# One Hymba-style encoder layer: the last MLP group by seven products, in the PSUM banks of the group in front of it

## The chip, the cores and the metric

The kernel runs on one NeuronCore of a Trainium2 chip. The metric is the device time of one execution in microseconds (us). The kernel before takes 780.66 us, the median of 3 runs (780.21 to 782.45).

## The reference, cut to what matters

The layer normalises x (512 tokens of 1024), projects it, runs two groups of attention heads, a cross-attention and an MLP, and normalises the result. The change touches only the second half of the MLP and the last norm:

```python
    u = rmsnorm(h, norm_ff_g[l]) @ w1[l]          # 512 x 4096
    h = h + jnp.square(jax.nn.relu(u)) @ w2[l]    # w2 is 4096 x 1024
return rmsnorm(h, final_norm_g)
```

## The kernel before

**Groups.** The hidden width of 4096 is cut into eight groups of 512 (`g` = 0 to 7, `NG` = 8). For a group, `mlp_up` makes four PSUM tiles of 128 hidden rows by 512 tokens, and `square` turns each into squared ReLU in SBUF (`sq`, two tiles of [128, 2, 512] per group). The way down multiplies these 512 hidden units by a 512 x 1024 piece of `w2` and adds the result to the residual, which is kept in four SBUF tiles `acc0` to `acc3` of 128 tokens by 1024.

**Numbers as high and low parts.** Every operand of a matmul is split in two: ACT writes a rounded copy (`hi`, line 166 for weights, `hidden_part` for the hidden side), DVE the remainder (`lo`, line 168). A product takes three matmuls: hi times hi, hi times lo, lo times hi (lines 1289 to 1291). The stationary operand is the hidden side (`hb`), the moving one the weight (`whd`, `wld`).

**Seven products instead of eight.** For groups 0 to 6 the way down is a 2 x 2 block product made with seven half-sized products (`PRODUCTS`, in the order "1", "2", "6", "5", "7", "3", "4") instead of eight. Its four weight blocks are loaded as `a1`, `c1`, `a2`, `b2`, `b1` into eight buffers that go round (`slots`, inside the tiles `wq0` and `wq1`), by DMAs of the SP queue. Sums of weight blocks are made by DMAs that add into SBUF (`add_weights`, on the POOL queue). Sums of hidden blocks are made on DVE (`hidden_sums`). One product is 12 matmuls of 128 x 512: two token halves `t`, two slices `k`, three matmuls. Its result goes through one of the banks U, Y and V (two of each), from which `add_to` adds it to `acc` on DVE.

**The last group.** Group 7 is done plainly: `hidden_plain` splits its four hidden slices, four weight blocks are split without sums, and `plain_down` (lines 1298 to 1307) makes, for each of four token blocks and each of two column halves, 12 matmuls. `last_block` follows a token block at a time: DVE adds the PSUM bank to `acc` (line 1319), ACT squares it and sums along the row (line 1320), POOL adds the two halves' sums and raises to the power -0.5 (lines 1325, 1331), ACT scales one half of the columns (line 1332), DVE the other (line 1334), and ACT and SP each send one half out. The last token block's second column half is done in two pieces of 256 columns.

**What sets the order.** PE's order is the order of the code. On the other engines the order is set when the program is built, from the place in the code, with the splits of weights moved ahead (`ahead(PW)`). At run time every engine takes its instructions strictly in that order, each waiting for its semaphores. `unit` keeps up to four split weight units ready: `whd` and `wld` have four buffers each, so the split of a unit waits until PE is done with the unit four before. The tiles of 4 KB per partition that hold `hb` and `acc` (`s4`) have twelve buffers, `k4` has four.

Of the kernel before, what the change touches and what calls it, by code (L numbers as in the profile page):

```python
# [16 lines left out]
P = 128  # L17
S = 512
# [24 lines left out]
def emit(  # L43
# [1102 lines left out]
    def up_units(g):  # L1146
        for j in range(2):
            spec = panel(w1, g * HG + j * WT)
            for n in range(2):

                def prep(g=g, j=j, n=n, spec=spec):
                    if (j, n) == (0, 0):
                        raws[g - 1] = down_raws(g - 1)
# [15 lines left out]
    def down_raws(g):  # L1169

        w = {}
        for n, name in enumerate(("a1", "c1", "a2", "b2", "b1") if g < NG - 1 else ("a1", "a2", "b2", "b1")):
            r, c = quad[name]
            w[name] = slots[(5 * g + n) % 8]
# [3 lines left out]
        if g < NG - 1:  # L1178
            add_weights(w["a2"], w["b2", "src"])
            add_weights(w["c1"], w["a2", "src"])  # L1180
        return w
# [4 lines left out]
    def down_units(g):  # L1186
        w = {}
        names = PRODUCTS if g < NG - 1 else ("a1", "a2", "b2", "b1")

        def prep(name, n):  # L1190
            if n == 0:
                w.update(raws.pop(g) if g in raws else down_raws(g))
            raw = w[RAW.get(name, name)]
# [8 lines left out]
        for n, name in enumerate(names):  # L1202
            unit_q.append((("d", g, name), lambda name=name, n=n: prep(name, n)))
# [47 lines left out]
    def hidden_plain(g, k):  # L1251
        src = sqs[g, k // 2][:, k % 2, :]
        hb = s4([2, S], f"hb{g}_{k}", R)
        ac.activation(hb[:, 0, :], src, AF.Copy)
        ve.tensor_tensor(hb[:, 1, :], src, f(hb[:, 0, :]), ALU.subtract)
        hbs[g, k] = hb

    def add_to(ps, rows, half, t, sign):
        a = acc[2 * rows + t][:, half * S : (half + 1) * S]
        if sign > 0:  # L1260
            ve.tensor_tensor(a, ps, a, ALU.add)
        else:
            ve.scalar_tensor_tensor(a, ps, -1.0, a, op0=ALU.mult, op1=ALU.add)
# [12 lines left out]
    def mlp_down(g):  # L1276
        banks = {}
        for name in PRODUCTS:
            whi, wlo = unit("d", g, name)
            bank, first_, goes = PLAN[name]  # L1280
            hb = hbs[g, name]
            for t in range(2):
                if first_:
                    banks[bank, t] = {"U": sc, "Y": tr, "V": mm}[bank](f"{bank}{g}{t}")
                ps = banks[bank, t]
                ts_ = slice(t * P, (t + 1) * P)
                for k in range(2):
                    hi, lo = hb[:, 0, k, ts_], hb[:, 1, k, ts_]
                    te.matmul(ps, hi, whi[:, k, :], start=first_ and k == 0, stop=False, skip_group_check=True)  # L1289
                    te.matmul(ps, hi, wlo[:, k, :], start=False, stop=False, skip_group_check=True)  # L1290
                    te.matmul(ps, lo, whi[:, k, :], start=False, stop=k == 1, skip_group_check=True)  # L1291
                for rows, half, sign in goes:
                    add_to(ps, rows, half, t, sign)
            if g + 1 < NG - 1:
                hidden_part(g + 1, name)
            elif PRODUCTS.index(name) < 4:
                hidden_plain(g + 1, PRODUCTS.index(name))

    def plain_down(ps, tb, wts, ns):
        ts_ = slice(tb * P, (tb + 1) * P)  # L1300
        for k in range(4):
            hb = hbs[NG - 1, k]
            whi, wlo = wts[k // 2]
            hi, lo = hb[:, 0, ts_], hb[:, 1, ts_]
            te.matmul(ps, hi, whi[:, k % 2, ns], start=k == 0, stop=False)
            te.matmul(ps, hi, wlo[:, k % 2, ns], start=False, stop=False)
            te.matmul(ps, lo, whi[:, k % 2, ns], start=False, stop=k == 3)

    def last_block(wts, tb, pieces):

        o = k4([D], f"fo{tb}")
        a = acc[tb]
        ms = sm(len(pieces), f"fm{tb}")
        part = None
        for n, (half, ns) in enumerate(pieces):
            ps = mm(f"y{half}{tb}_{ns.start}")[:, ns]
            plain_down(ps, tb, wts[half], ns)
            cs = slice(half * S + ns.start, half * S + ns.stop)
            ve.tensor_tensor(a[:, cs], ps, a[:, cs], ALU.add)
            ac.activation(o[:, cs], a[:, cs], AF.Square, scale=1.0 / 32.0, accum_out=ms[:, n : n + 1])  # L1320
            if part is None:
                part = ms[:, n : n + 1]
            else:
                e = sm(1, f"fe{tb}{n}")
                gp.tensor_scalar(e, ms[:, n : n + 1], part, EPS if n == len(pieces) - 1 else 0.0, op0=ALU.add, op1=ALU.add)
                part = e
        h0, h1 = slice(0, S), slice(S, D)
        ag = t2(f"fa{tb}")
        gp.tensor_tensor(ag, a[:, h0], gfin[0], op=ALU.mult)
        r = sm(1, f"fr{tb}")  # L1330
        gp.tensor_tensor(r, part, mhalf[:, 0:1], op=ALU.pow)
        ac.activation(o[:, h0], ag, AF.Identity, scale=r)
        ac.dma_start(out[tb * P : (tb + 1) * P, h0], o[:, h0])
        ve.scalar_tensor_tensor(o[:, h1], a[:, h1], r, gfin[1], op0=ALU.mult, op1=ALU.mult)
        nc.sync.dma_start(out[tb * P : (tb + 1) * P, h1], o[:, h1])

    def mlp_up_group(g):
        for j in range(2):
            if g < 2:
                wt = next_panel()  # L1340
                if (g, j) == (0, 0):
                    raws[0] = down_raws(0)
# [3 lines left out]
            else:  # L1346
                wt = tuple(list(x) for x in zip(*(unit("u", g, j, n) for n in range(2))))
            yield from mlp_up(g, j, wt)

    for g in range(NG):  # L1350
        if g >= 2:
            up_units(g)
        if g >= 1:
            down_units(g - 1)
    down_units(NG - 1)
# [26 lines left out]
    wts = [[got["a1"], got["b1"]], [got["a2"], got["b2"]]]  # L1382
    halves = [(0, slice(0, S)), (1, slice(0, S))]
    quarters = [(0, slice(0, S)), (1, slice(0, WT)), (1, slice(WT, S))]
    for tb in range(NT):
        last_block(wts, tb, halves if tb < NT - 1 else quarters)
# [28 lines left out]
```

## Time and profile before

| | |
|---|---|
| median of 3 runs | 780.66 us |
| the profiled execution | 779.9 us |
| its span, first to last instruction | 778.2 us |
| granted TensorE clock, mean | 0.998 |
| products of group 6 start | 728.53 us |
| plain matmuls of group 7 start | 747.57 us |
| last matmul starts | 770.51 us |

The profile has one execution. Engines are PE (matmul), PEld (load of the stationary operand), DVE, ACT, POOL, SP. In a timeline a row gives start, duration, engine, line of the kernel, operation, output and inputs, count, and in brackets the idle time of that engine before it with what ended it. A matmul's row of 128 x 512 lasts 0.39 us because matmuls overlap; the distance between two starts is what one costs.

### The profile page before, as it was taken

Reading aid. Unit: us, or ns where it says so; the run is one execution under the profiler, and the core shown is the slowest. Engines: PE = TensorE matmul, PEld = TensorE weight load, DVE = VectorE, ACT = ScalarE, POOL = GpSimd, SP = SyncE. Lnnn points to the kernel's source line nnn. Section 1 sums busy time; section 2 is a strip of 40 time slices with the busy share of each in tenths; the row PEclk is TensorE's granted clock in tenths of the full one; section 3 lists DMA queues with packets and bytes.
Section 4 is the critical chain, followed back from the end, with each engine's and each line's share of the span. In section 5 each row is a group of like instructions: output and inputs, shape, how many; then the busy total and the mean of one; then the engine's idle time right before and its main releaser. Section 6 shows DMA issues by size and latency. Waiting matters only on the chain.

```text
span 778.2 us, 11540 instructions
## 1 busy us (share of the span) xinstructions
PE 767.7 (99%) x4380; PEld 655.1 (84%) x4380; DVE 517.7 (67%) x839; ACT 366.3 (47%) x626; POOL 187.4 (24%) x259
## 2 busy tenths in 40 slices
PE   8999999999999999999999999999999999999996
PEld 6889998988989988888888888888888888888875
DVE  4747755587587656655548656949595868778662
ACT  5655555676474533244434244444353535344433
POOL 7107432424344024410016510101001010100013
PEclk9999999999999999999999999999999999999999
DMA  8553322232544343222113596575758485754302
GB/s 237 196 123 112 97 56 82 81 110 83 163 134 128 121 161 95 94 83 81 55 55 100 205 253 147 147 177 155 177 158 188 140 201 144 194 132 119 71 4 106
DMA packets 80777, 100.43 MB, mean 129 GB/s; under 512 B 4513, under 2 KB 62410, under 8 KB 80722
## 3 DMA queue, kind: packets, MB, share of 16 engines
q1 hardware_dynamic: 72002, 76.08, 32.0%
q0 software_dynamic: 8128, 22.57, 13.6%
q10 hardware_dynamic: 592, 1.05, 0.4%
q8 instruction: 34, 0.56, 0.3%
q14 instruction: 21, 0.17, 0.1%
HBM read 88.14 MB, written 4.21 MB: 119 GB/s over the span
## 4 chain that ended last, share of the span: by engine, by line
PE 94%; DVE 2%; ACT 1%; DMA 1%; POOL 1%; issue 1%; SPq 0%; POOLq 0%; ACTq 0%
PE u L227 7%; PE u L228 7%; PE u L229 7%; PE U L1290 3%; PE U L1289 3%; PE U L1291 3%; PE xq L227 2%; PE xw L227 2%; PE xw L229 2%; PE xq L228 2%; PE xq L229 2%; PE xw L228 2%; PE wo L229 2%; PE wo L227 2%; PE wo L228 2%; PE Y L1290 2%
## 5 line engine op out<-in xcount | busy, mean ns | idle before, releaser
L168 DVE TENSOR_TENSOR wld<-wq,whd 128x1024 fp32r<-128x1024 f32 x49 | 59.7, 1219 | 24.0 <-ACT whd L166 23.9
L228 PE MATMUL u<-x_lo,whu 128*128 128x512 f32 x192 | 74.7, 389 | 0.0
L229 PE MATMUL u<-x_hi,wlu 128*128 128x512 f32 x192 | 74.7, 389 | 0.0
L227 PE MATMUL u<-x_hi,whu 128*128 128x512 f32 x192 | 74.7, 389 | 0.0
L166 ACT ACTIVATE whd<-wq 128x1024 fp32r<-128x1024 f32 x49 | 51.0, 1051 | 23.6 <-PE u L228 23.6
L166 ACT ACTIVATE whu<-wru 128x1024 fp32r<-128x1024 f32 x24 | 25.3, 1053 | 56.9 <-DMA wru<-in_w_dram 56.9
L168 DVE TENSOR_TENSOR wlu<-wru,whu 128x1024 fp32r<-128x1024 f32 x24 | 29.3, 1220 | 26.7 <-ACT whu L166 26.7
L1167 POOL DMA_DIRECT2D wq<-in_w_dram x14 | 17.0, 1217 | 116.6 <-DMA wq<-in_w_dram 113.8
L1167 POOL DMA_DIRECT2D wq<-wq x14 | 12.3, 877 | 134.4 <-DVE wld L168 95.9
L1289 PE MATMUL U<-whd,hb 128*128 128x512 f32 x112 | 43.6, 389 | 0.0
L1290 PE MATMUL U<-wld,hb 128*128 128x512 f32 x112 | 43.6, 389 | 0.0
L1291 PE MATMUL U<-whd,hb 128*128 128x512 f32 x112 | 43.6, 389 | 0.0
L227 PEld LDWEIGHTS u<-x_hi,whu 128*128 128x128 f32 x192 | 36.0, 188 | 7.5
L229 PEld LDWEIGHTS u<-x_hi,wlu 128*128 128x128 f32 x192 | 36.0, 188 | 7.5
L228 PEld LDWEIGHTS u<-x_lo,whu 128*128 128x128 f32 x192 | 36.0, 188 | 7.4
L1227 ACT ACTIVATE sq<-ur 128x512 f32<-128x512 f32 x32 | 19.9, 624 | 29.1 <-DVE ur L1224 29.1
L1224 DVE SCALAR_TENSOR_TENSOR ur<-u,rbc 128x512 f32<-128x512 f32 x32 | 21.9, 688 | 17.5 <-PE u L229 17.5
L862 POOL TENSOR_SCALAR bi<-nF,Ft 128x128 f32<-128x128 f32 (+3 forms) x32 | 21.7, 678 | 43.9 <-PE pv L905 16.8
L879 ACT ACTIVATE bi<-bi,mx 128x128 f32<-128x128 f32 (+3 forms) x32 | 17.9, 560 | 21.9 <-DVE mx L877 21.8
L1289 PEld LDWEIGHTS U<-whd,hb 128*128 128x128 f32 x112 | 21.0, 188 | 4.4
L1291 PEld LDWEIGHTS U<-whd,hb 128*128 128x128 f32 x112 | 21.0, 188 | 4.4
L1290 PEld LDWEIGHTS U<-wld,hb 128*128 128x128 f32 x112 | 21.0, 188 | 4.3
(950 smaller groups left out, 2452.6 us busy)
## 6 DMA issues: line engine op xcount, KB each, us to landing
wq<-in_w_dram SPq DMA_DIRECT2D x39, 512.0 KB, 3.7
wru<-in_w_dram SPq DMA_DIRECT2D x24, 512.0 KB, 3.8
wq<-in_w_dram POOLq DMA_DIRECT2D x14, 512.0 KB, 8.4
wq<-wq POOLq DMA_DIRECT2D x14, 512.0 KB, 4.6
xTd<-xT POOLq DMA_DIRECT2D x4, 512.0 KB, 3.0
nF<-Fd POOLq DMA_DIRECT2D x8, 256.0 KB, 4.3
hT<-xTd POOLq DMA_DIRECT2D x4, 512.0 KB, 4.7
xt<-in_x_dram SPq DMA_DIRECT2D x3, 512.0 KB
```

The costliest lines, as they stand in the source:

```text
L166: ac.activation(hi, raw, AF.Copy)
L168: ve.tensor_tensor(lo, raw, f(hi), ALU.subtract)
L227: te.matmul(ps, wh, hi, start=n_ == 0, stop=False)
L228: te.matmul(ps, wh, lo, start=False, stop=False)
L229: te.matmul(ps, wl, hi, start=False, stop=n_ == KC - 1)
L862: gp.tensor_scalar(bi[:, 0:n], fF[h][:, 0:n], -1.0, Ft[:, tb, h : h + 1], op0=ALU.mult, op1=ALU.add)
L1167: gp.dma_start(raw.rearrange("p (k n) -> p k n", k=2), src, accum_op=ALU.add)
L1224: ve.scalar_tensor_tensor(u, ps, 0.0, rbc2, op0=ALU.max, op1=ALU.mult)
L1227: ac.activation(sqs[g, j][:, i, :], u, AF.Square)
L1289: te.matmul(ps, hi, whi[:, k, :], start=first_ and k == 0, stop=False, skip_group_check=True)
L1290: te.matmul(ps, hi, wlo[:, k, :], start=False, stop=False, skip_group_check=True)
L1291: te.matmul(ps, lo, whi[:, k, :], start=False, stop=k == 1, skip_group_check=True)
```

## The change

Group 7 is made by the same seven products as the others, and it is woven into group 6: after each product of group 6 comes the same product of group 7, into the same PSUM banks, and `add_to` runs only after group 7's. The five weight blocks of group 7 are loaded by `down_raws(NG - 1)`; two of them go into free `k4` tiles. `last_block` is replaced by `finish`, which is called when an (token block, column half) piece of `acc` has had its last addition: after product "2" (blocks 0 and 1, columns 0 to 511), "7" (blocks 2 and 3, columns 512 to 1023), "3" (blocks 0 and 1) and "4" (blocks 2 and 3). A first call makes the sum of squares and the product with the norm's gain for that half; a second call adds the other half's squares, makes the row's factor and sends both halves out. For blocks 2 and 3 the second sum of squares is made on DVE (`tensor_tensor_reduce`) instead of ACT. The very last matmuls (product "4" of group 7, second token half) are done in two pieces of 256 columns. In all groups the addition of `a2` to `a1` is issued with product "1" instead of "2".

```diff
-    def down_raws(g):
-        w = {}
-        for n, name in enumerate(("a1", "c1", "a2", "b2", "b1") if g < NG - 1 else ("a1", "a2", "b2", "b1")):
...
+    def load_raws(g, names):
+        w = raws.setdefault(g, {})
+        for name in names:
             r, c = quad[name]
-            w[name] = slots[(5 * g + n) % 8]
+            n = 5 * g + RAWS.index(name)
+            w[name] = slots[n % 8] if n < 38 else k4([D], f"wq{n}")
...
-            if name == "2":
-                for to, of in (("a1", "a2"), ("b1", "a1")):
-                    add_weights(w[to], w[of].rearrange("p (k n) -> p k n", k=2))
+            if name in ("1", "2"):
+                to, of = (("a1", "a2"), ("b1", "a1"))[int(name) - 1]
+                add_weights(w[to], w[of].rearrange("p (k n) -> p k n", k=2))
...
-    def mlp_down(g):
+    def mlp_down(gs):
+        end = gs[-1] == NG - 1
         banks = {}
-        for name in PRODUCTS:
-            whi, wlo = unit("d", g, name)
+        for n, name in enumerate(PRODUCTS):
             bank, first_, goes = PLAN[name]
...
+            for g in gs:
+                whi, wlo = unit("d", g, name)
+                hb = hbs[g, name]
+                for t in range(2):
+                    if first_ and g == gs[0]:
+                        banks[bank, t] = {"U": sc, "Y": tr, "V": mm}[bank](f"{bank}{g}{t}")
+                    ps = banks[bank, t]
+                    ts_ = slice(t * P, (t + 1) * P)
+                    last = (g, name, t) == (NG - 1, PRODUCTS[-1], 1)
+                    for ns in (slice(0, WT), slice(WT, S)) if last else (slice(0, S),):
+                        for k in range(2):
+                            hi, lo = hb[:, 0, k, ts_], hb[:, 1, k, ts_]
+                            begin = first_ and g == gs[0] and k == 0
...
+                        for rows, half, sign in goes if g == gs[-1] else ():
+                            add_to(ps, rows, half, t, sign, ns)
+                            if end and (name, rows) in FINAL:
+                                finish(2 * rows + t, half, ns)
+            if not end:
+                hidden_part(gs[0] + 1, name)
+            elif n + 1 < len(PRODUCTS):
+                hidden_part(NG - 1, PRODUCTS[n + 1])
+    FINAL = (("2", 0), ("7", 1), ("3", 0), ("4", 1))
+    fin = {}
+    def finish(tb, half, ns):
+        a = acc[tb]
+        cs = slice(half * S + ns.start, half * S + ns.stop)
+        if tb not in fin:
+            e = sm(1, f"fe{tb}")
+            ac.activation(t2(f"fj{tb}"), a[:, cs], AF.Square, scale=1.0 / 32.0, accum_out=e)
+            gp.tensor_scalar(e, e, 1.0, EPS, op0=ALU.mult, op1=ALU.add)
+            ag = t2(f"fa{tb}")
+            gp.tensor_tensor(ag, a[:, cs], gfin[half], op=ALU.mult)
+            fin[tb] = [e, cs, ag, None]
+            return
...
+        if tb < 2:
+            ac.activation(o[:, cs], a[:, cs], AF.Square, scale=1.0 / 32.0, accum_out=v)
+            v0, v = v, sm(1, f"fw{tb}")
+            gp.tensor_scalar(v, v0, e, 0.0, op0=ALU.add, op1=ALU.add)
+        else:
+            ve.tensor_tensor_reduce(out=o[:, cs], in0=a[:, cs], in1=a[:, cs], scale=1.0 / D, scalar=e, op0=ALU.mult, op1=ALU.add, accum_out=v)
+        fin[tb][0] = v
+        if ns.stop < S:
+            ag2 = t2(f"fb{tb}")
+            gp.tensor_tensor(ag2[:, ns], a[:, cs], gfin[half][:, ns], op=ALU.mult)
...
+        r = sm(1, f"fr{tb}")
+        gp.tensor_tensor(r, v, mhalf[:, 0:1], op=ALU.pow)
+        def scale():
...
+            ac.activation(o[:, cs0], ag, AF.Identity, scale=r)
+            ac.dma_start(out[rows, cs0], o[:, cs0])
...
+            if ns.start:
+                p0 = slice(half * S, half * S + ns.start)
+                ve.tensor_scalar(o[:, p0], fin["piece"][:, 0 : ns.start], r, None, op0=ALU.mult)
+            ve.scalar_tensor_tensor(o[:, cs], a[:, cs], r, gfin[half][:, ns], op0=ALU.mult, op1=ALU.mult)
+            nc.sync.dma_start(out[rows, hs_], o[:, hs_])
...
+                if (g, j) == (NG - 1, 0):
+                    down_raws(NG - 1)
...
+        hidden_sums(g)
         if g < NG - 1:
-            hidden_sums(g)
-        mlp_down(g - 1)
-    got = {n: unit("d", NG - 1, n) for n in ("a1", "a2", "b2", "b1")}
...
-    for tb in range(NT):
-        last_block(wts, tb, halves if tb < NT - 1 else quarters)
+            mlp_down((g - 1,))
+    hidden_part(NG - 1, PRODUCTS[0])
+    mlp_down((NG - 2, NG - 1))
```

**ACT, end of its queue.** The rows name the tile written, then the tiles read; the number after `hb` or `whd` is group and product, `fo`, `fa`, `fr` and `fv` carry the token block. Before, the hidden parts are all split ahead of the first row of the final norm:

```order
L1254 ACTIVATE hb7_3_7059<-sq71_6942 128x512
L166 ACTIVATE whd64_7039<-wq0_4782 128x1024
L166 ACTIVATE whd7a1_7066<-wq0_4782 128x1024
L166 ACTIVATE whd7a2_7084<-wq1_4783 128x1024
L166 ACTIVATE whd7b2_7102<-wq1_4783 128x1024
L166 ACTIVATE whd7b1_7120<-wq1_4783 128x1024
L1320 ACTIVATE fo0_7124,fm0_7125<-acc0_4498 128x512 x2
```

After, at the same end of ACT's queue:

```order
L166 ACTIVATE whd74_7209<-wq39_6854 128x1024
L1315 ACTIVATE fj2_7188,fe2_7187<-acc2_4500 128x512
L1315 ACTIVATE fj3_7201,fe3_7200<-acc3_4501 128x512
L1326 ACTIVATE fo0_7232,fv0_0_7233<-acc0_4498 128x512
L1342 ACTIVATE fo0_7232<-fa0_7066,fr0_7237 128x512
L1326 ACTIVATE fo1_7250,fv1_0_7251<-acc1_4499 128x512
L1343 DMA out_0_dram<-fo0_7232 128x512
L1342 ACTIVATE fo1_7250<-fa1_7079,fr1_7255 128x512
L1249 ACTIVATE hb74_7261<-sq71_6952 128x512
L1343 DMA out_0_dram<-fo1_7250 128x512
```

The high part of group 7's product "4" (`hb74`) now stands behind the second sums of squares and the scalings of token blocks 0 and 1.

**DVE, end of its queue.** Before, three rows for each column half and token block; the last two blocks end so:

```order
L1334 SCALAR_TENSOR_TENSOR fo2_7208<-acc2_4500,fr2_7244,gfin1_4779 128x512
L1319 TENSOR_TENSOR acc3_4501<-y03_0_7252,acc3_4501 128x512
L1319 TENSOR_TENSOR acc3_4501<-y13_0_7267,acc3_4501 128x256
L1319 TENSOR_TENSOR acc3_4501<-y13_256_7284,acc3_4501 128x256
L1334 SCALAR_TENSOR_TENSOR fo3_7250<-acc3_4501,fr3_7303,gfin1_4779 128x512
```

After, the last rows are these (ISA is `tensor_tensor_reduce`, and the 128x1 row behind it reads its sum):

```order
L1259 TENSOR_TENSOR acc2_4500<-U60_6998,acc2_4500 128x512
L1259 TENSOR_TENSOR acc3_4501<-U61_7005,acc3_4501 128x256
L1330 ISA fo2_7283,fv2_0_7284<-acc2_4500,fe2_7187 128x512
L1330 ISA fv2_0_7284 128x1
L1330 ISA fo3_7295,fv3_0_7296<-acc3_4501,fe3_7200 128x256
L1330 ISA fv3_0_7296 128x1
L1259 TENSOR_TENSOR acc3_4501<-U61_7005,acc3_4501 128x256
L1348 SCALAR_TENSOR_TENSOR fo2_7283<-acc2_4500,fr2_7286,gfin0_4778 128x512
L1330 ISA fo3_7295,fv3_256_7307<-acc3_4501,fv3_0_7296 128x256
L1330 ISA fv3_256_7307 128x1
L1347 TENSOR_SCALAR fo3_7295<-fb3_7298,fr3_7309 128x256
L1348 SCALAR_TENSOR_TENSOR fo3_7295<-acc3_4501,fr3_7309,gfin0_4778 128x256
```

The sums of squares of blocks 2 and 3 are now on DVE, and the scaling of block 2 stands between the two pieces of block 3. Right ahead of the first of these rows stands the low part of `hb74` (line 1253), and ahead of that the scalings of blocks 0 and 1 (line 1348).

**POOL, from the weight sums of groups 5 to 7 to the first row of the norm.** `in_w2_dram` is an addition from HBM, the others add one SBUF tile to another. Before:

```order
L1167 DMA wq1_4783<-in_w2_dram 128x2x512
L1167 DMA wq0_4782<-in_w2_dram 128x2x512
L1167 DMA wq0_4782<-wq0_4782 128x1024
L1167 DMA wq1_4783<-wq0_4782 128x1024 x2
L1167 DMA wq0_4782<-wq1_4783 128x1024
L1329 TENSOR_TENSOR fa0_7158<-acc0_4498,gfin0_4778 128x512
```

After:

```order
L1167 DMA wq0_4782<-wq0_4782 128x1024
L1167 DMA wq1_4783<-wq0_4782 128x1024
L1167 DMA wq1_4783<-in_w2_dram 128x2x512 x2
L1167 DMA wq1_4783<-wq0_4782 128x1024
L1167 DMA wq0_4782<-wq1_4783 128x1024 x2
L1167 DMA wq39_6854<-wq0_4782 128x1024
L1318 TENSOR_TENSOR fa0_7066<-acc0_4498,gfin0_4778 128x512
```

Two additions from HBM for group 7 now stand ahead of group 6's addition of `a2` to `a1`, and two of group 7's own stand among and behind group 6's.

More of the change, by code (lines that the diff above doesn't have):

```diff
@@ L1249, in hidden_part, with add_to @@
         hbs[g, name] = hb
[L1251 to L1259, printed above, removed]
+    def add_to(ps, rows, half, t, sign, ns):
+        a = acc[2 * rows + t][:, half * S + ns.start : half * S + ns.stop]
         if sign > 0:
[L1261 removed]
+            ve.tensor_tensor(a, ps[:, ns], a, ALU.add)
         else:
[L1263 removed]
+            ve.scalar_tensor_tensor(a, ps[:, ns], -1.0, a, op0=ALU.mult, op1=ALU.add)
     PLAN = {
@@ L1299, in plain_down @@
[L1299 to L1311, printed above, removed]
-        a = acc[tb]
[L1313 to L1329, printed above, removed]
-        r = sm(1, f"fr{tb}")
[L1331 to L1335, printed above, removed]
```

75 lines of the change are left out of this document (37 added, 38 removed).

## The prediction, made before the changed kernel ran

> **What bounds the kernel now.** I read the page first, for the engine that sets the end:
>
> ```profile
> span 778.2 us, 11540 instructions
> ...
> PE 767.7 (99%) x4380; PEld 655.1 (84%) x4380; DVE 517.7 (67%) x839; ACT 366.3 (47%) x626; POOL 187.4 (24%) x259
> ...
> PE 94%; DVE 2%; ACT 1%; DMA 1%; POOL 1%; issue 1%; SPq 0%; POOLq 0%; ACTq 0%
> ```
>
> PE is busy 99% of the span and makes 94% of the chain that ended last, so time is won by fewer matmuls, by fewer waits of PE, or behind the last matmul. Nothing ahead of group 7 changes but the moment of some DMAs, so I read the two last stages, the seven products of group 6 and the plain matmuls of group 7, in the table of busy time by stretch:
>
> ```profile
> core 0: us, PE busy (x) PEld busy (x) DVE busy (x) ACT busy (x) POOL busy (x), PEclk, DMA share, GB/s
> 728.53:747.57 19.04, 19.04 (x85) 15.77 (x84) 18.40 (x24) 9.51 (x11) 0.00 (x0) 1.00 0.09 29
> 747.57:770.63 23.06, 22.31 (x109) 18.51 (x107) 9.46 (x14) 8.80 (x20) 7.95 (x11) 1.00 0.17 66
> ```
>
> Group 6 is 84 matmuls of 512 columns in 19.04 us without a gap: 0.2267 us each, 2.72 us for a product of 12. Group 7 is 84 matmuls of 512 and 24 of 256 columns. The timeline of PE gives the price of the short ones and shows a wait:
>
> ```profile
> 748.93 0.46 PE L1305 MATMUL y<-whd7b,hb 128*128 128x512 f32 x1
> 750.14 0.50 PE L1306 MATMUL y<-wld7b,hb 128*128 128x512 f32 x1 [0.75 <-DVE wld7b L168]
> ...
> 753.93 0.39 PE L1307 MATMUL y<-whd7b,hb 128*128 128x512 f32 x1
> ...
> 770.39 0.28 PE L1306 MATMUL y<-wld7b,hb 128*128 128x256 f32 x1
> 770.51 0.28 PE L1307 MATMUL y<-whd7b,hb 128*128 128x256 f32 x1
> ```
>
> A short one costs 770.51 - 770.39 = 0.12 us. The work of this stage is thus 84 x 0.2267 + 24 x 0.12 = 21.92 us; it took 23.06, so 1.14 us are the wait for the last weight block's low part at 750.14 and the restart behind it.
>
> **The change, step by step.**
>
> *Matmuls.* Group 7 becomes 78 matmuls of 512 and 12 of 256 columns: 17.68 + 1.44 = 19.12 us for 21.92, **-2.80 us**. The wait at 750.14 comes from needing all four weight blocks within one token block; in the new order one block is needed every 2.72 us, so it goes: **-1.14 us**. Without a new wait PE would end at 728.53 + 162 x 0.2267 + 12 x 0.12 = 766.69, instead of 770.63.
>
> *Splits and sums of weights.* ACT and DVE split 14 units instead of 11 for the two groups, and there are five more DMAs (one load, four additions). The grouped rows and the DMA part of the page:
>
> ```profile
> L168 DVE TENSOR_TENSOR wld<-wq,whd 128x1024 fp32r<-128x1024 f32 x49 | 59.7, 1219 | 24.0 <-ACT whd L166 23.9
> ...
> L166 ACT ACTIVATE whd<-wq 128x1024 fp32r<-128x1024 f32 x49 | 51.0, 1051 | 23.6 <-PE u L228 23.6
> ...
> wq<-in_w_dram POOLq DMA_DIRECT2D x14, 512.0 KB, 8.4
> wq<-wq POOLq DMA_DIRECT2D x14, 512.0 KB, 4.6
> ```
>
> In 5.44 us of PE (one product of each group) DVE has two splits (2.44), one hidden part and two additions (0.68 each): 4.5 us. It had 18.40 of 19.04 us in group 6 and PE did not wait, so it hides. A unit's split may begin when PE leaves the unit four before and is wanted 8.2 us later; working through the queues row by row I find each weight ready at least 3 us early. The timeline of POOL gives the moments of the weight additions:
>
> ```profile
> 662.80 1.21 POOL L1167 DMA_DIRECT2D wq<-in_w_dram  x1 [17.84 <-DMA wq<-in_w_dram]
> 665.39 1.21 POOL L1167 DMA_DIRECT2D wq<-in_w_dram  x1 [1.38 <-DMA wq<-in_w_dram]
> ...
> 717.52 0.86 POOL L1167 DMA_DIRECT2D wq<-wq  x1 [32.25 <-DVE wld L168]
> ```
>
> One group lasts 180 x 0.2267 = 40.8 us. Group 7's two additions from HBM come one group after 662.80 and 665.39, at about 704 and 706, and land 8.4 us later, ahead of the POOL row of 717.52 that they precede. Group 7's `a2` to `a1` follows at about 721 and lands by 726; ACT wants it at 734 and PE at 742. I cost all this at nothing; if that cover is gone, PE waits as long as the data is late.
>
> *The new wait.* In the order of ACT and DVE the hidden part "4" of group 7 stands behind the final norm's second half of blocks 0 and 1. How long that takes is seen in the first block of before, in the timelines of DVE, ACT and POOL:
>
> ```profile
> 754.35 0.69 DVE L1319 TENSOR_TENSOR acc<-y,acc 128x512 f32<-128x512 f32 x1 [2.06 <-PE y L1307]
> 755.08 0.63 ACT L1320 ACTIVATE fo<-acc 128x512 f32<-128x512 f32 x1 [2.02 <-DVE acc L1319]
> 755.91 0.31 POOL L1325 TENSOR_SCALAR fe<-fm 128x1 f32<-128x1 f32 x1 [2.24 <-ACT fo L1320]
> 756.30 0.59 POOL L1331 TENSOR_TENSOR fr<-fe,mhalf 128x1 f32<-128x1 f32 x1
> 756.92 0.72 ACT L1332 ACTIVATE fo<-fa,fr 128x512 f32<-128x512 f32 x1 [1.12 <-POOL fr L1331]
> ...
> 731.51 0.63 ACT L1254 ACTIVATE hb<-sq 128x512 fp32r<-128x512 f32 x1 [1.42 <-PE U L1291]
> 732.18 0.69 DVE L1255 TENSOR_TENSOR hb<-sq,hb 128x512 fp32r<-128x512 f32 x1
> ```
>
> From start to start: last matmul to addition 0.42 (753.93 to 754.35), to square 0.73, to POOL's sum 0.83, to the power 0.39, to the scaling 0.62. Product "3" of group 7 is the twelfth of the stage and starts at 728.53 + 11 x 2.72 = 758.45; its sixth matmul starts at 759.58, block 0's addition at 760.00, its square at 760.73, its scaling at 762.57. ACT is held at that scaling; block 1's square, whose input has long been there, follows it at 763.25 (0.68 later, between ACT's rows of 0.63 and 0.72), and block 1's scaling 0.83 + 0.39 + 0.62 later at 765.09. Only then comes the hidden part: high 765.72 to 766.35, low on DVE to 767.07. PE wants the high part at 728.53 + 13 x 2.72 = 763.89 and the low part two matmuls later, at 764.34. It waits 2.5 us, does two matmuls, waits again: 767.10 - 764.34 = 2.76, and 0.1 for the restart, **+2.85 us**. Bounds: 2.4 if ACT's and POOL's rows overlap a little more, 3.3 if POOL's small rows take 0.2 longer beside DVE. PE then ends at 769.54, 1.09 earlier than before.
>
> *Behind the last matmul.* Before, in the timeline of DVE:
>
> ```profile
> 770.82 0.42 DVE L1319 TENSOR_TENSOR acc<-y,acc 128x256 f32<-128x256 f32 x1 [1.01 <-PE y L1307]
> 772.92 0.75 DVE L1334 SCALAR_TENSOR_TENSOR fo<-acc,fr,gfin 128x512 f32<-128x512 f32 x1 [1.67 <-POOL fr L1331]
> ```
>
> With E = 770.63 for PE's end, the last scaled half is ready at 773.67 = E + 3.04. After, two token blocks end together instead of one, and DVE makes their sums of squares. `tensor_tensor_reduce` and the rows beside it stand in the grouped rows (its name there is CUSTOM_DVE_ANT_0):
>
> ```profile
> L877 DVE CUSTOM_DVE_ANT_0 bi<-ps,bi 128x512 f32<-128x512 f32 x8 | 5.5, 686 | 0.2 <-POOL bi L863 0.2
> L877 DVE CUSTOM_DVE_ANT_0 bi<-ps,bi 128x256 f32<-128x256 f32 x8 | 3.4, 419 | 1.7 <-PE ps L872 1.6
> L877 DVE DVE_READ_ACCUMULATOR2_ANT mx<- 128x1 f32 x32 | 2.6, 82 | 0.0
> L1062 DVE TENSOR_SCALAR xp<-xp,xd 128x256 f32<-128x256 f32 x16 | 4.9, 351 | 0.3
> L684 POOL TENSOR_TENSOR mov<-mov,F 128x256 f32<-128x256 f32 x14 | 13.8, 1007 | 17.1 <-PE lv L658 17.1
> L1329 POOL TENSOR_TENSOR fa<-acc,gfin 128x512 f32<-128x512 f32 x4 | 5.2, 1294 | 33.4 <-DVE acc L1319 33.4
> L999 POOL TENSOR_TENSOR ssq<-ssq,wosq 128x512 f32<-128x512 f32 x7 | 13.5, 1925 | 0.5
> ```
>
> DVE in its order: addition of block 2 from E - 1.25, of block 3's first piece from E - 0.53, squares of block 2 to E + 0.55, of the first piece to E + 0.97, addition of the second piece to E + 1.4. The scaling of block 2 waits for POOL: 128 x 256 product from E - 0.1 (1.01 by the row of that size, 0.65 by half the 1294), then the power (0.6), so E + 1.5 to E + 2.25; it stands ahead of the last squares, which end at E + 2.7. Power to E + 3.3, then a scaling of 256 columns by 0.35 and one of about 0.45: E + 4.1. That is **+1.06 us**. The two stores that follow have the same size as before.
>
> The sum against the profiled execution: -2.80 - 1.14 + 2.85 + 1.06 = -0.03 us.
>
> POOL's product of 512 columns takes 1294 ns in the tail and 1925 beside more DVE work. If block 3's small product and DVE's squares of block 2 take turns, up to 0.7 is added; I put in 0.2 of it. So +0.2 in all: 780.1 for 779.9 of the profiled execution. That execution lies 0.76 under the median, and I carry the difference: **780.8 us**. [...]
>
> **The rivals.**
>
> *The hidden part "4" comes in time.* Then PE does not wait and the time is 780.8 - 2.85 = 777.9, faster. For it: 0.63 of ACT work is all that is missing, and its input is made at the start of the stage. Against it: the row stands behind the scaling of block 1 in ACT's queue, and the chain of rows to that scaling (760.00 to 765.09) has no slack. 0.17.
>
> *The clock falls in the new gap.* Windows of the end of before, with the granted clock as the third number from the right:
>
> ```profile
> 774.00:774.50 0.50, 0.00 (x0) 0.00 (x0) 0.00 (x0) 0.00 (x0) 0.00 (x0) 1.00 0.00 0
> 774.50:775.00 0.50, 0.00 (x0) 0.00 (x0) 0.00 (x0) 0.00 (x0) 0.00 (x0) 0.71 0.92 352
> 775.00:775.50 0.50, 0.00 (x0) 0.00 (x0) 0.00 (x0) 0.00 (x0) 0.00 (x0) 0.50 0.99 377
> ```
>
> 0.71 over that half us is a fall to 0.50 at 774.7, 3.9 us after the last matmul's end at 770.79. The new gap is some 2.5 us; if the clock fell in it, the 18 matmuls behind it (6 x 0.2267 + 12 x 0.12 = 2.80 us) would take twice as long: 780.8 + 2.8 = 783.6, slower. It decides from a gap of 3.9 us, or less if the count begins elsewhere. 0.06. [...]
>
> *Group 7's weights pace the stage*, so that the saved matmuls bring nothing. DVE's 18.40 of 19.04 us speak for it, as does POOL's queue, where an addition from HBM now stands ahead of one that group 6 needs; the slack of 3 us at each split and 8 at each addition speaks against. Lost would be the 2.80 and perhaps as much again in waits: 783 to 786, slower, or a small loss within the bound. 0.14.
>
> **How the numbers follow.** The forecast has 0.63, with 779.9 to 781.7 as its own range (wait 2.4 to 3.3, tail 0.2 less to 0.5 more). 0.3% is 2.3 us, about what a measurement can tell from no change: 778.3 and 783.0 are the limits. Faster: 0.15 of the first rival and 0.02 of the forecast, 0.17. Slower: 0.06, 0.10 of the last rival and 0.03 of the forecast, 0.19. Same: 0.64. The range takes in the first rival and the near half of the slower ones: 777.6 to 783.2.
>
> **What would show it.** Right: 2.72 us from product to product with no gap up to the fourteenth; there a gap of about 2.5 us in front of the first matmul of "4" of group 7, ended by ACT's `hb` (line 1249), and a small one ended by DVE's; clock 1.00 behind it; PE's end near 769.5; the last scaling ready 4.1 us later. No gap there, or one in an earlier product ended by a weight (lines 166, 168), would prove me wrong; so would a tail of under 3.5 or over 5 us.

## The result and the profile after

The changed kernel takes 784.63 us (median of 13 runs, 781.11 to 786.2) beside 781.4 us of the kernel before (13 runs, 779.83 to 783.23): a ratio of 1.0039, 95% interval 1.0029 to 1.0048, so some 3 us slower. Two more comparisons gave 1.0048 (1.0031 to 1.0065) and 1.0045 (1.0030 to 1.0060). The profiled execution has 783.27 us, a span of 781.5 and a mean clock of 0.994.

The page of the changed kernel, its span and its busy time:

```profile
span 781.5 us, 11524 instructions
...
PE 765.5 (98%) x4362; PEld 652.1 (83%) x4362; DVE 524.6 (67%) x848; ACT 368.8 (47%) x626; POOL 195.0 (25%) x265
```

PE has 2.2 us less work than before, and the span is 3.3 us longer: PE waits for more than the change took away. To see where, I cut the span at the first matmul of the seven products of group 5 and at that of the woven stage (groups 6 and 7), in the timeline of PE, first before, then after:

```profile
687.73 0.39 PE L1289 MATMUL U<-whd,hb 128*128 128x512 f32 x1
...
728.53 0.39 PE L1289 MATMUL U<-whd,hb 128*128 128x512 f32 x1
```

```profile
688.98 0.39 PE L1293 MATMUL U<-whd,hb 128*128 128x512 f32 x1
...
731.57 0.39 PE L1293 MATMUL U<-whd,hb 128*128 128x512 f32 x1
```

Between the two lie 180 matmuls, of the down products of group 5 and the up matmuls of group 7. They took 40.80 us before (180 x 0.2267, no gap) and 42.59 after. So the +3.3 us are +1.25 ahead of group 5, **+1.79 in group 5** and +0.26 from the start of the woven stage to the end (49.67 before, 49.93 after).

**Ahead of group 5** PE's code is the same; only the place of one weight addition differs. The difference arises at the first tiles of x, in the timelines of PE before and after (the next group of this line starts at 9.65 and at 10.92 us, already 1.27 apart):

```profile
5.98 1.11 PE L399 MATMUL xn<-ident,xt 128*128 128x128 f32 x4 [0.55 <-DMA xt<-in_x_dram]
```

```profile
7.55 1.01 PE L399 MATMUL xn<-ident,xt 128*128 128x128 f32 x4 [2.56 <-DMA xt<-in_x_dram]
```

In the ten other profiles of this study this wait was 0.59, 0.76, 0.90, 0.95, 2.23, 2.31, 2.54, 2.75, 3.04 and 3.52 us: 0.59, 2.56 and 3.52 for the changed kernel alone. It is drawn anew in each execution and says nothing of the change, so profiles are compared by their stages below.

**In group 5.** The timelines of SP, POOL, ACT and DVE of the changed kernel, around the start of that group's products:

```profile
679.15 0.97 SPq L1178 DMA_DIRECT2D wq<-in_w_dram  x2
694.92 11.70 SPq L1178 DMA_DIRECT2D wq<-in_w_dram  x5
...
680.44 0.90 POOL L1167 DMA_DIRECT2D wq<-wq  x1 [12.76 <-DVE wld L168]
690.24 0.86 POOL L1167 DMA_DIRECT2D wq<-wq  x1 [8.89 <-DMA wq<-wq]
...
689.76 2.01 ACT L166 ACTIVATE whd<-wq 128x1024 fp32r<-128x1024 f32 x2 [4.67 <-DMA wq<-wq]
...
690.86 1.22 DVE L168 TENSOR_TENSOR wld<-wq,whd 128x1024 fp32r<-128x1024 f32 x1 [6.43 <-ACT whd L166]
```

and the same addition in the timelines of POOL, ACT and DVE of before:

```profile
679.16 0.90 POOL L1167 DMA_DIRECT2D wq<-wq  x1 [12.56 <-DVE wld L168]
684.41 0.86 POOL L1167 DMA_DIRECT2D wq<-wq  x1 [4.34 <-DMA wq<-wq]
...
684.99 1.06 ACT L166 ACTIVATE whd<-wq 128x1024 fp32r<-128x1024 f32 x1 [1.14 <-PE u L228]
...
686.08 1.23 DVE L168 TENSOR_TENSOR wld<-wq,whd 128x1024 fp32r<-128x1024 f32 x1 [2.89 <-ACT whd L166]
```

SP issues the loads of group 7's blocks `b2` and `b1` from 679.15 on, because their `k4` tiles are free; the next loads in its queue have to wait for tiles (14.7 us) and follow from 694.92. POOL issues group 5's addition of `a2` to `a1` 1.3 us later; it now lands after 8.89 us of POOL's waiting, not 4.34. ACT waits for it ("<-DMA wq<-wq", before it waited for PE only), DVE for ACT. Counted from the first product, DVE's split is 3.5 us later than before (690.86 - 688.98 = 1.88, before 686.08 - 687.73 = -1.65). DVE has no room to catch up in this stage. The table of busy time for 19.04 us of it, before (from 0.2 us behind the first matmul) and after (from 2.2 us behind it, when DVE is at work again):

```profile
core 0: us, PE busy (x) PEld busy (x) DVE busy (x) ACT busy (x) POOL busy (x), PEclk, DMA share, GB/s
687.90:706.94 19.04, 19.04 (x85) 15.77 (x85) 18.83 (x27) 9.93 (x13) 0.00 (x0) 1.00 0.48 144
```

```profile
691.21:710.25 19.04, 18.25 (x77) 13.95 (x76) 19.04 (x27) 9.74 (x13) 1.68 (x2) 1.00 0.60 173
```

DVE was busy 18.83 of 19.04 us before and is busy all the time after, so what it is late is passed on to PE: the second row has 8 matmuls fewer, 8 x 0.2267 = 1.8 us. PE's timeline has two waits that were not there:

```profile
695.16 0.47 PE L1293 MATMUL U<-whd,hb 128*128 128x512 f32 x1 [0.59 <-DVE acc L1259]
...
701.10 0.47 PE L1293 MATMUL U<-whd,hb 128*128 128x512 f32 x1 [0.21 <-DVE acc L1261]
```

They name DVE's sums into `acc`, two engines behind the DMA that is the cause. The rest of the 1.8 us are the slower restarts behind these waits (the next matmul starts 0.31 and 0.30 us later, where 0.23 is usual) and delays too short to be listed as one (0.08 us each at 704.03, 704.34, 706.96 and 707.27).

**In the woven stage.** Thirteen of its fourteen products run without a gap, and the fourteenth waits, in PE's timeline:

```profile
769.40 0.50 PE L1293 MATMUL U<-whd,hb 128*128 128x512 f32 x1 [2.31 <-ACT hb L1249]
769.74 0.40 PE L1294 MATMUL U<-wld,hb 128*128 128x512 f32 x1
770.13 0.50 PE L1295 MATMUL U<-whd,hb 128*128 128x512 f32 x1
...
772.54 0.39 PE L1293 MATMUL U<-whd,hb 128*128 128x256 f32 x1 [0.52 <-DVE acc L1259]
...
773.24 0.28 PE L1295 MATMUL U<-whd,hb 128*128 128x256 f32 x1
```

and the end of DVE's timeline:

```profile
771.36 1.12 DVE L1259 TENSOR_TENSOR acc<-U,acc 128x512 f32<-128x512 f32 x2 [1.29 <-PE U L1295]
...
773.08 0.94 DVE L1330 CUSTOM_DVE_ANT_0 fo<-acc,fe 128x256 f32<-128x256 f32 x1
...
775.13 0.48 DVE L1330 CUSTOM_DVE_ANT_0 fo<-acc,fv 128x256 f32<-128x256 f32 x1
...
776.55 0.48 DVE L1348 SCALAR_TENSOR_TENSOR fo<-acc,fr,gfin 128x256 f32<-128x256 f32 x1
```

The gap of 2.31 us is the one forecast. The wait of 0.52 us at 772.54 is not: the second piece of 256 columns writes the PSUM bank from which DVE still reads the first piece, until 772.48.

This profile does not hold the whole loss. Its traces explain 1.79 + 0.26 = 2.05 us, the three medians say 3.0 to 3.7. The rest was found by a second profile, below.

### The profile page after: what moved, and what is told of

The parts are those of the page before. It is cut to its first block, busy times and chain, and to the rows that moved or that the text cites. A ratio compares the mean times of both kernels' runs of the same rounds, so it can differ in the third digit from the quotient of the medians.

```text
span 781.5 us, 11524 instructions
## 1 busy us (share of the span) xinstructions
PE 765.5 (98%) x4362; PEld 652.1 (83%) x4362; DVE 524.6 (67%) x848; ACT 368.8 (47%) x626; POOL 195.0 (25%) x265
## 4 chain that ended last, share of the span: by engine, by line
PE 86%; DVE 3%; issue 3%; DMA 3%; ACT 2%; POOL 1%; SPq 0%; POOLq 0%; DVEq 0%; ACTq 0%
PE u L227 7%; PE u L228 6%; PE u L229 6%; PE U L1293 3%; PE U L1295 3%; PE U L1294 3%; PE xq L227 2%; PE xw L227 2%; PE xw L229 2%; PE xq L228 2%; PE xq L229 2%; PE xw L228 2%; PE wo L227 2%; PE wo L228 2%; PE wo L229 2%
## 5 line engine op out<-in xcount | busy, mean ns | idle before, releaser
L168 DVE TENSOR_TENSOR wld<-wq,whd 128x1024 fp32r<-128x1024 f32 x56 | 69.7, 1245 | 27.7 <-ACT whd L166 27.6
L166 ACT ACTIVATE whd<-wq 128x1024 fp32r<-128x1024 f32 x56 | 58.3, 1053 | 33.4 <-PE u L228 17.6
L1293 PE MATMUL U<-whd,hb 128*128 128x512 f32 (+1 forms) x130 | 50.6, 390 | 3.6 <-ACT hb L1249 2.3
L1167 POOL DMA_DIRECT2D wq<-in_w_dram x16 | 19.4, 1215 | 131.9 <-DMA wq<-in_w_dram 119.8
L1295 PE MATMUL U<-whd,hb 128*128 128x512 f32 (+1 forms) x130 | 50.3, 387 | 0.0
L1294 PE MATMUL U<-wld,hb 128*128 128x512 f32 (+1 forms) x130 | 50.2, 386 | 0.0
L1167 POOL DMA_DIRECT2D wq<-wq x16 | 14.0, 877 | 125.4 <-DVE wld L168 85.7
L1293 PEld LDWEIGHTS U<-whd,hb 128*128 128x128 f32 x130 | 24.4, 188 | 10.1 <-ACT hb L1249 2.7
L1295 PEld LDWEIGHTS U<-whd,hb 128*128 128x128 f32 x130 | 24.4, 188 | 5.4 <-DVE hb L1253 0.4
L1294 PEld LDWEIGHTS U<-wld,hb 128*128 128x128 f32 x130 | 24.4, 188 | 4.9
```

The costliest lines, as they stand in the source:

```text
L166: ac.activation(hi, raw, AF.Copy)
L168: ve.tensor_tensor(lo, raw, f(hi), ALU.subtract)
L1167: gp.dma_start(raw.rearrange("p (k n) -> p k n", k=2), src, accum_op=ALU.add)
L1293: te.matmul(ps[:, ns], hi, whi[:, k, ns], start=begin, stop=False, skip_group_check=True)
L1294: te.matmul(ps[:, ns], hi, wlo[:, k, ns], start=False, stop=False, skip_group_check=True)
L1295: te.matmul(ps[:, ns], lo, whi[:, k, ns], start=False, stop=k == 1, skip_group_check=True)
```

## The experiments

My theory after the first traces: the step that failed is "five more DMAs cost nothing"; two early loads make group 5 late by 1.7 us. Rivals: the loss lies in the start, or in the woven stage. Each ratio is to the kernel before, run beside it on the same chip, with its 95% interval.

### Late loads of two blocks

```diff
-        load_raws(g, RAWS)
+        load_raws(g, RAWS if g < NG - 1 else RAWS[:3])
...
             square(*up)
+        if g == NG - 1:
+            load_raws(g, ("b1", "b2"))
         hidden_sums(g)
```

The tiles now come free in group 5's products, and SP issues the two loads behind the last up weights.

> The changed kernel, but group 7's raw blocks b1 and b2 are loaded behind all the up weights of group 7 (into buffers that come free in group 5's products), not 27 us ahead of their neighbours. Theory (the early loads slow the weight addition of group 5, which makes VectorE and then PE late by 1.7 us): 1.7 us less than the changed kernel, about 782.9 against 784.6, or some 1.5 above the kernel before; PE's waits for VectorE's sums at 687 to 707 us vanish, and the addition issued near 680 us lands after about 4.4 us, not 8.9. Rival (the loss is in the start, where the code is the same, and in the last stage): 784.6, no change, though the addition lands early.

Measured: 782.1 us, ratio 1.0015 (1.0002 to 1.0028). Against the changed kernel's 1.0039 that is 1.9 us less. The timelines of POOL, ACT and PE show the cover back: the addition lands after 4.22 us, ACT waits for PE again, and the 180 matmuls take 731.01 - 690.21 = 40.80 us, as before.

```profile
681.74 0.90 POOL L1167 DMA_DIRECT2D wq<-wq  x1 [12.76 <-DVE wld L168]
686.86 0.86 POOL L1167 DMA_DIRECT2D wq<-wq  x1 [4.22 <-DMA wq<-wq]
...
687.47 1.06 ACT L166 ACTIVATE whd<-wq 128x1024 fp32r<-128x1024 f32 x1 [1.14 <-PE u L228]
...
690.21 0.39 PE L1293 MATMUL U<-whd,hb 128*128 128x512 f32 x1
...
731.01 0.39 PE L1293 MATMUL U<-whd,hb 128*128 128x512 f32 x1
```

### The kernel before with two more loads, and with four

```diff
+                if (g, j) == (NG - 1, 0):
+                    for r in range(2):
+                        extra = k4([D], f"extra{r}")
+                        src = w2[...].rearrange("(k p) n -> p k n", p=P)
+                        nc.sync.dma_start(extra.rearrange("p (k n) -> p k n", k=2), src)
             yield from mlp_up(g, j, wt)
```

The second kernel runs the loop over (0, 1, 0, 1), so that each tile is loaded twice.

> The kernel before with one part of the change alone: two more loads of 512 KB that nothing reads, at the place in SP's queue at which the changed kernel loads b1 and b2 of group 7. Theory (these loads are what costs): 1.5 to 1.9 us above the kernel before, about 783.1 against 781.4, with group 5's addition landing after about 9 us and waits of PE for VectorE's sums in group 5. Rival (the cost is elsewhere): 781.4, within 0.3 us of the kernel before.

> The kernel before with four extra loads of 512 KB that nothing reads, at the place of the two of the earlier run (two at once, and two more behind them). Theory (extra loads beside group 5's weight additions make VectorE and PE late): 2.5 to 4 us above the kernel before, about 784, with PE's waits for VectorE's sums in group 5 longer than the 1.4 us that the profile with two loads showed. Rival (the loss with two loads, 0.6 us by the medians, is not really there): below 1 us.

Measured: 781.54 us, ratio 1.0008 (0.9995 to 1.0020), with two; 781.7 us, 1.0018 (1.0009 to 1.0027), with four. POOL's timeline with two loads, and those of SP and POOL with four:

```profile
681.16 0.90 POOL L1167 DMA_DIRECT2D wq<-wq  x1 [12.96 <-DVE wld L168]
690.70 0.86 POOL L1167 DMA_DIRECT2D wq<-wq  x1 [8.64 <-DMA wq<-wq]
```

```profile
679.85 5.54 SPq L1353 DMA_DIRECT2D extra<-in_w_dram  x3
695.90 0.46 SPq L1353 DMA_DIRECT2D extra<-in_w_dram  x1
...
681.13 0.90 POOL L1167 DMA_DIRECT2D wq<-wq  x1 [12.80 <-DVE wld L168]
690.82 0.86 POOL L1167 DMA_DIRECT2D wq<-wq  x1 [8.78 <-DMA wq<-wq]
```

Two loads that nothing reads bring the late addition into the kernel before, with the same 0.7 and 0.2 us of PE waiting for DVE, and 42.64 us for the 180 matmuls (+1.84). The median of that run alone would not carry it: 0.6 us, where I had expected 1.5 to 1.9. With four loads it is 1.4 us, and the interval lies above 1. That four would cost twice as much was wrong: the addition lands after 8.78 us as with two, and the 180 matmuls take 42.62. But not all four ran beside it: SP's row of three lasts 5.54 us, where that of two took 0.97, so the third, into the tile of the first, went out some 5 us later, and the fourth at 695.90, behind the addition. Two that start 1.3 us ahead of the addition were enough for the cost, and a third 5 us later added nothing.

### The hidden part of the last product made earlier

```diff
-            elif n + 1 < len(PRODUCTS):
-                hidden_part(NG - 1, PRODUCTS[n + 1])
+            elif n < 5:
+                for following in PRODUCTS[n + 1 : n + 2 + n // 4]:
+                    hidden_part(NG - 1, following)
```

> The changed kernel, but the hidden part of group 7's product 4 is made together with that of product 3, ahead of the first norm steps of rows 0 and 1 in ScalarE's and VectorE's queues. Theory (the gap of 2.3 us ahead of the first matmul of 4 of group 7 is the whole price of the new wait, and nothing else is late there): 2.2 to 2.6 us less than the changed kernel, about 782.2, gap gone, the tail behind the last matmul unchanged near 3.7. Rival (something else is late next: the norm of rows 0 and 1 or the sums of product 3 are pushed into the tail): 0 to 1.5 less, and a tail of 4.5 us or more.

Measured: 779.84 us, ratio 0.9988 (0.9977 to 1.0000): 4.0 us less than the changed kernel, more than either theory gave. PE's timeline has no gap ahead of the fourteenth product; what is left is the wait of the second piece:

```profile
765.57 0.39 PE L1295 MATMUL U<-whd,hb 128*128 128x512 f32 x1
765.79 0.39 PE L1293 MATMUL U<-whd,hb 128*128 128x512 f32 x1
...
768.71 0.39 PE L1293 MATMUL U<-whd,hb 128*128 128x256 f32 x1 [0.69 <-DVE acc L1259]
...
769.41 0.28 PE L1295 MATMUL U<-whd,hb 128*128 128x256 f32 x1
```

Its woven stage and tail (what follows the last matmul) take 47.27 us for 49.93 (777.7 - 730.43), so its trace explains 2.7 us. The other 1.3 us are missing in the trace of the changed kernel too: that raised the rival that I had given 0.06, the clock.

### The changed kernel again

> The changed kernel once more, beside the next three. The traces explain about 2.0 us of its loss (1.7 in group 5, 0.3 in the last stage); the medians say 3. Theory (the gap ahead of product 4 of group 7 lowers PE's clock in part of the executions, and PE then works its last 18 matmuls at half speed): some 3 us above the kernel before as at first, a mean granted clock near 0.993 over the executions against 0.997 of the kernel before, and a profile that has either full clock or half clock behind the gap. Rival (the first median was an accident of the start, whose length varies by 2.5 us from one profile to the next): 2 us or less above the kernel before.

Measured: 784.67 us, ratio 1.0048 (1.0031 to 1.0065), mean clock over its executions 0.9932 for 0.9970 of before. This profile caught what the first did not. PE's timeline behind the gap, where two starts of 512 columns lie 0.43 us apart instead of 0.23, and windows of half a us (the clock is the third number from the right):

```profile
771.19 0.50 PE L1293 MATMUL U<-whd,hb 128*128 128x512 f32 x1 [2.32 <-ACT hb L1249]
...
772.32 0.63 PE L1293 MATMUL U<-whd,hb 128*128 128x512 f32 x1
772.75 0.63 PE L1294 MATMUL U<-wld,hb 128*128 128x512 f32 x1
```

```profile
771.50:772.00 0.50, 0.50 (x3) 0.08 (x1) 0.36 (x1) 0.00 (x0) 0.00 (x0) 1.00 0.94 365
772.00:772.50 0.50, 0.50 (x2) 0.40 (x3) 0.00 (x0) 0.00 (x0) 0.00 (x0) 0.66 0.98 381
...
775.00:775.50 0.50, 0.08 (x1) 0.00 (x0) 0.38 (x2) 0.00 (x0) 0.00 (x0) 0.50 0.00 0
775.50:776.00 0.50, 0.40 (x3) 0.40 (x4) 0.50 (x2) 0.00 (x0) 0.38 (x1) 0.92 0.00 0
```

0.66 over half a us is a fall at 772.16, and 0.92 a return at 775.58: the clock is halved for 3.42 us, beginning 1.0 us after PE is back at work. Woven stage and tail take 784.6 - 733.35 = 51.25 us, against 49.93 with full clock: a fall costs 1.3 us.

### The gap filled

```diff
+                if (g, name) == (NG - 1, "4"):
+                    spare = mm("spare")
+                    w3, h3 = units["d", g, "3"][0], hbs[g, "3"]
+                    for r in range(9):
+                        te.matmul(spare, h3[:, 0, 0, 0:P], w3[:, 0, :], start=r == 0, stop=r == 8, skip_group_check=True)
                 hb = hbs[g, name]
```

With the late loads (`late_warm`), and in the changed kernel as it is (`after_warm`, with the changed kernel once more beside it, `after_third`):

> The late loads again, and nine more matmuls of 128x512 (2.0 us) into a PSUM bank that nothing reads, in the gap ahead of product 4 of group 7, so that PE stands still for 0.3 us there instead of 2.3. The waits and the data are the same as in the run with the late loads alone (782.1, mean clock 0.9938). Theory (in part of the executions the gap costs clock): 1.0 us less, about 781, within 0.4 us of the kernel before, mean clock 0.9955 or more. Rival (the gap costs its 2.3 us and no clock): 782.1 or a little more, clock unchanged.

> The changed kernel with its early loads as they are, and the nine matmuls that nothing reads in the gap ahead of product 4 of group 7. The profile of the second run of the changed kernel showed the clock at 0.54 and 0.61 behind that gap and 1.4 us more up to the last matmul. Theory (the clock falls behind the gap in most executions): 1.0 to 1.5 us less than the changed kernel beside it, mean clock 0.0015 to 0.0025 higher, and full clock behind the gap in the profile. Rival (it falls in few): 0 to 0.4 us less, the mean clock within 0.001.

> The changed kernel beside the run with the nine matmuls. Both theories: 3 to 3.7 us above the kernel before, mean clock near 0.993. The profile shows one more draw of the start (0.5 to 3.5 us of PE waiting for the first tiles so far) and of the clock behind the gap.

Measured: 780.66 us, ratio 1.0010 (0.9999 to 1.0021) with late loads, mean clock 0.9956; 782.38 us, 1.0022 (1.0012 to 1.0032) in the changed kernel, mean clock 0.9959; 783.88 us, 1.0045 (1.0030 to 1.0060) and 0.9933 for the changed kernel beside it. PE's timeline of the filled gap in the changed kernel:

```profile
765.33 2.20 PE L1286 MATMUL spare<-whd,hb 128*128 128x512 f32 x9
...
767.81 0.50 PE L1298 MATMUL U<-whd,hb 128*128 128x512 f32 x1 [0.28 <-ACT hb L1249]
```

The wait for the hidden part is as long as it was (2.70 us from the last matmul of the product before to the first of "4", 765.11 to 767.81, as from 766.70 to 769.40 without the nine), and woven stage and tail take 50.03 us, as long as in the profile with full clock. Still 1.8 us went (the two intervals together allow 0.4 to 3.2), and the mean clock rose by 0.0026. With the late loads the same step gave 0.4 us, from 1.0015 to 1.0010, within its uncertainty; the clock rose there too, by 0.0018.

How often the clock falls can be estimated from the mean clock of each execution. In the profiles (that with four more loads left aside) it holds a fall behind the last matmul, which delays no matmul: with the gap, open or filled, half of the last 5.5 to 6.0 us (from 775.70 to 781.5 in the first profile of the changed kernel), which makes 0.996 without another fall. A fall of 3.4 us to half takes 0.0022 more. A mean of 0.994 or less was measured in 21 of 25 executions of the changed kernel and in 9 of 12 with the late loads, but in 5 of 24 with the gap filled and 5 of 29 with the hidden part made early. So, as an estimate from these counts, the gap brings a fall in some three of four executions, 1.0 us at 1.3 each. Of the four profiles with the gap only the second of the changed kernel shows it (the 0.994 of the first is from another fall, at the start, from 7.70 to 11.11 us).

### Both edits, and the last product whole

`late_hb4` has the late loads and the early hidden part. `late_hb4_whole` has in addition:

```diff
-                    for ns in (slice(0, WT), slice(WT, S)) if last else (slice(0, S),):
+                    for ns in (slice(0, S),):
```

> Both edits in the changed kernel: late loads of b1 and b2, and the hidden part of 4 made early. Theory (the two prices are independent and add up): 1.7 + 2.4 = 4.1 us less than the changed kernel, about 780.5, so 0.9 below the kernel before. Rival (the start or the stage holds the loss, and only one edit pays): 782 to 783.

> The two edits that paid (late loads, early hidden part of 4), and the last product in one piece of 512 columns instead of two of 256. Theory (the second piece waits 0.5 us for VectorE to read the first from the same bank, which eats what the pieces save behind the last matmul): last matmul 0.6 to 0.8 us earlier, tail 0.4 to 0.8 longer, 778.3 within 0.4. Rival (the pieces pay in spite of the wait): 0.5 to 1.0 above the run with the pieces.

Measured: 778.34 us, ratio 0.9964 (0.9952 to 0.9976), and 777.26 us, 0.9962 (0.9948 to 0.9975). Either beats both kernels: some 2.8 us below the kernel before, 6 below the changed one. That is more than the 4.1 that I had added up for both edits, and the fall of the clock behind the gap, some 1.0 us, was not in that sum. By the medians the two can't be told apart; by the traces the whole product is 0.5 us shorter from the start of the woven stage to the end (46.73 for 47.24 us). The end of DVE's timeline, with pieces and whole:

```profile
767.67 1.02 DVE L1259 TENSOR_TENSOR acc<-U,acc 128x512 f32<-128x512 f32 x2
...
772.75 0.48 DVE L1349 SCALAR_TENSOR_TENSOR fo<-acc,fr,gfin 128x256 f32<-128x256 f32 x1
```

```profile
767.69 0.68 DVE L1259 TENSOR_TENSOR acc<-U,acc 128x512 f32<-128x512 f32 x1
...
771.92 0.75 DVE L1349 SCALAR_TENSOR_TENSOR fo<-acc,fr,gfin 128x512 f32<-128x512 f32 x1 [0.66 <-POOL fr L1339]
```

In the traces the pieces lose more on the wait for the bank (0.69 us) and on small instructions (the squares of the last half block take 0.95 + 0.48 us for 0.75) than they win by starting early.

All profiles by stage, in us (the 180 matmuls of group 5 and the next up part; woven stage and tail to the end of the span; in the kernels made from before, the last two stages and the tail):

| kernel | 180 matmuls | last stage and tail |
|---|---|---|
| before | 40.80 | 49.67 |
| changed, three profiles | 42.59, 42.85, 42.61 | 49.93, 51.25 (clock fell), 50.01 |
| late loads | 40.80 | 49.99 |
| before, two and four more loads | 42.64, 42.62 | 49.30, 49.45 |
| early hidden part | 42.84 | 47.27 |
| gap filled: late loads, changed | 40.80, 42.53 | 50.00, 50.03 |
| both edits, in pieces and whole | 40.80, 40.80 | 47.24, 46.73 |

Every kernel with the two early loads has 42.5 to 42.9 us in the first column, every one without has 40.80.

## Why the prediction was wrong

I forecast 780.8, no change; the kernel is 3 to 3.7 us slower, outside the range. Point by point:

- **Matmuls, -2.80, and the old wait, -1.14: right.** From 731.57 the thirteenth product ends at 766.93, 13 x 2.72 us, without a gap, and no weight is waited for in the stage.
- **The DMAs at nothing: the step that failed**, with the sentence that nothing ahead of group 7 changes but the moment of some DMAs. It is that moment that costs: the two loads are not among the five more that I counted, the kernel before has them too, only later. I looked for the cost of these transfers where their data is wanted, where there is slack of several us, and not at what they run beside when they are issued. I placed the additions of group 7 in time row by row, and not the loads; two loads without a buffer to wait for were free to go 16 us ahead of the next in the queue (679.15 and 694.92), into a stage in which DVE had 0.2 us of 19 to spare. Cost 1.8 us in the trace, 1.9 by the run that takes it away. None of the signs that I named looks at group 5.
- **The new wait, +2.85: right.** The first matmul of "4" starts 769.40 - 766.93 = 2.47 us late, the third at 770.13, which is 2.75 us later than without a wait. The small wait for DVE shows in front of the load of the stationary operand (PEld, 0.4 us for line 1253).
- **"Clock 1.00 behind it": wrong in most executions** (some three of four, by the estimate above). Here the rival to which I gave 0.06 came true beside the forecast: a fall costs 1.3 us in the trace (51.25 for 49.93), and filling the gap saved 1.8 (0.4 to 3.2). My 2.8 for it was too much, since the clock fell at 772.16, 1.0 us after PE's start at 771.19, and was back at 775.58, ahead of PE's last six matmuls (from 775.60). I had set the point from which it decides at 3.9 us, from one fall at the end of the kernel before; that was an estimate, and the runs show no such point. One gap of 2.32 us was followed by half clock and three of 2.31 to 2.33 us were not, and at the end of the changed kernel's first profile the fall comes 2.2 us behind the last matmul (773.52 to 775.70).
- **The tail, E + 4.1: a little too long.** With E = 773.24 + 0.12 = 773.36 the last scaling is ready at 777.03, E + 3.67. DVE's squares of 256 columns took 0.94 us where they began beside POOL's product (772.57 to 773.74 us) and 0.48 without it, so the delay that I priced at 0.2 was there, with 0.46; but PE's end came later by the wait of the second piece, and DVE had done the more before it.
- **The second piece's wait for the bank: not foreseen**, 0.52 us and the restart, 0.77 together (the last matmul at 773.24, without the wait at 771.75 + 6 x 0.12 = 772.47). The two pieces share no column, and still PE starts only at 772.54, just behind the end of DVE's row at 772.48; with the last product whole this wait is not there.

The sum for the woven stage and the tail, +0.2 us, was met at +0.26 in the profile with full clock, but in part by luck: PE's end came 0.31 us earlier than before and not 1.09, and from there to the last scaling it took 0.63 us more and not 1.06 and 0.2. The two errors cancel. (The range of the forecast has a slip without consequence: 780.8 - 0.45 - 0.2 is 780.15, not 779.9.) The loss of 3 us is 1.8 where I had put nothing and about 1 from the clock. The rival on group 7's weights named nearly the right size for another place: these weights made group 5 late, not their own stage.

What stays open: why two loads from HBM make an addition from SBUF to SBUF last 8.6 to 8.9 us instead of 4.2 to 4.3 (the DMA engines are busy throughout, with a share of 0.95 to 1.15 in windows of 1 us from 681 to 687 us, but no less during the short addition of before, 0.94 to 1.09 from 679 to 683), what decides whether a gap of this length halves the clock, and in how many executions it does exactly.

## What to carry to other kernels

A load that waits for no buffer goes when its queue comes to it, here 16 us ahead of the next (679.15 and 694.92); ask what runs at that moment, not when its data is wanted, and look there for the engine without slack (DVE, busy 18.83 of 19.04 us). A gap of PE is priced with what follows it: 2.32 us of standing still were followed by 3.42 us of half clock in one profile, and gaps as long by none in three others, so one profile can miss it; the mean clock of all executions, set beside that of a kernel without the gap, did not (0.9932 for 0.9970). Put the small preparation of the last product ahead of the norm steps that nothing waits for.

## What the runs showed of the hardware

- In group 5 POOL waited 4.22 and 4.34 us for an addition of 512 KB from SBUF to SBUF beside which no load started (late loads, before), and 8.64, 8.78 and 8.89 us for one behind two loads of 512 KB from HBM that started 1.3 us ahead of it (before with two and with four more loads, changed).
- The clock was halved for 3.42 us behind 2.32 us of PE standing still, and not in three other executions with gaps of 2.31, 2.31 and 2.33 us: the length alone did not decide. At the start of the changed kernel's first two profiles it fell at waits of 2.56 and 3.52 us (at 7.70 and 7.58), for 3.4 and 6.8 us.
- A clock of 1.00 in the windows need not be full speed at the start of the span: in the kernel before, matmuls of 512 columns start 0.43 us apart there (8.28, 8.71, 9.14 us), as in the half clock above, and the windows from 8 to 10 us read 1.00.
- The wait for the first tiles of x lasted from 0.55 to 3.52 us in twelve profiles of the same code.
